# The convolution's second column group: gate and b tiles by seven products, and the mixed operands' slices asked for sooner

## The chip, the cores and the metric

The kernel runs on one core of a Trainium2 chip. The metric is the device time of one execution in microseconds; a comparison takes the median of several runs. The engines are named as the profile names them: PE (matrix engine), DVE (vector), ACT (scalar), POOL (GpSimd) and SP (which only issues transfers here).

## The reference

Two layers on a residual stream x of 1024 tokens by 1024 features. The first, the one touched here, is a gated short convolution; the second is a dilated attention with three groups of heads and is left as it is.

```python
def short_conv_mixer(h, w_in, w_conv, w_out):
    S = h.shape[1]
    proj = h @ w_in                                   # (S, 4*2048)
    b_gate, c_gate, u, z = jnp.split(proj, 4, axis=-1)
    v = c_gate * u
    vp = jnp.pad(v, ((0, 0), (CONV_K - 1, 0), (0, 0)))
    conv = sum(w_conv[k] * vp[:, k:k + S] for k in range(CONV_K))
    y = b_gate * conv * jax.nn.silu(z)
    return y @ w_out
...
x = x + short_conv_mixer(rms_norm(x, conv_norm), ...)
x = x + dilated_attention_mixer(rms_norm(x, attn_norm), ...)
```

## The kernel before

Everything is computed transposed, features on the 128 partitions and tokens along a row, in two halves of 512 tokens (`hf`). The 2048 columns of the convolution are 16 column groups `e` of 128, and each group has four weight tiles `k`: 0 is u, 1 is the c gate, 2 is z (the SiLU gate) and 3 is b. One weight tile is 128x1024: 1024 input features, 128 columns.

**Precision.** A float32 operand is kept as a high and a low part. A weight tile half goes through `split_w` (L156 to L160): ACT copies the high part (L158), DVE subtracts to get the low part (L159). PE then does three matmuls of 512 columns for each 128x128 block: high by high, high by low, low by high.

**Plain products.** `products(k, hf)` (L361) takes a whole weight tile against one half of the tokens: 8 feature blocks by 3 = 24 matmuls (L368 to L370). So a weight tile takes 48, and a pair of them 96.

**Seven products.** `strassen` takes two weight tiles (a pair) as a 2 by 2 block matrix (upper and lower features, first and second tile) and the tokens likewise, and forms the four results from seven products of 12 matmuls each (L295, L297, L298): 84. For this `prepare` (L256) forms four mixed weights on POOL (L270) and splits seven, and four token operands are mixed as well. Their blocks are `blkd` (T1), `blkc` (T2), `blke` (T3) and `blkf` (T4), each of four slices `i`; plain operands stay in `blka`, `blkb`, `blkf` and `blkg`, so T4 takes a buffer that the plain products of the second half read. The products run in the order 1, 2, 4 (of the pair before), 6, 5, 3 (of the pair before), 7. Product 1 reads `blka`, 2 `blkb`, 6 `blkc`, 5 `blkd`, 7 `blke`. Products 1, 6, 7 and 4 accumulate in one PSUM bank, and ACT copies that bank (L303) after products 1 and 6 before the next one adds to it.

**Mixed operands.** `mixed(T)` (L190) is a generator. Each of its first four steps asks SP for four slices of x (L195) and forms slice `i` of T1, T2 and T3 on DVE and ACT (L201 to L214); the last one splits the four slices of T4. So it must be advanced five times before the seven products may begin.

**Order.** PE's order is that of the code (`manual_schedule`), ACT's too up to the end of group 0. The other queues are set by a scheduler that works with due times; each engine then executes its queue in order. Group 0 is done plainly, mixed with the loading of x and the row statistics (`row_stats`, `row_spread`: an inverse square root by small DVE rows, L63 to L67, then transposes on PE). Group 1 is done plainly too, while `mixed` is advanced; from group 2 on, all pairs run by seven products. `evac` takes a plain result: k = 0 and 1 give v, k = 2 the gate, k = 3 the taps of the convolution and `close` (L353 to L358), which multiplies by b and by the gate and sends the result to HBM.

**Buffers that couple the queues.** Raw weights have two (`wr`), so SP's issue of a weight waits until the tile two before is split. Split halves have eight (`ws`), mixed weights three (`sr`), 128x512 work tiles twelve (`f`), taps three (`g`).

Of the kernel before, what the change touches and what calls it, by code (L numbers as in the profile page):

```python
# [26 lines left out]
NE = E // P  # L27
# [8 lines left out]
def trunk(ctx: ExitStack, tc: tile.TileContext, a, out):  # L36
# [89 lines left out]
    def half(hf):  # L126
        return slice(hf * HALF, hf * HALF + HALF)

    with tc.tile_pool(name="wq", bufs=1) as wq, tc.tile_pool(name="sle", bufs=1) as sle, \
# [11 lines left out]
        def ftile():  # L141
            t = fp.tile([P, HALF], F32, name="f", tag="f", bufs=12)
            return t

        def gtile():
            t = cp.tile([P, HALF], F32, name="g", tag="g", bufs=3)
            return t
# [42 lines left out]
        def mixed(T):  # L190


            def x_tile(hf, kt):
                t = ftile()
                nc.sync.dma_start(t, a["x"][hf, kt])  # L195
                return t

            def put(n, i, t):
                if i == 0:
                    T[n] = block(" dcef"[n])  # L200
                nc.scalar.activation(T[n][:, i, 0], t, AF.Copy)  # L201
                nc.vector.tensor_tensor(T[n][:, i, 1], t, T[n][:, i, 0].bitcast(F32), op=OP.subtract)

            fourth = []
            for i in range(4):
                a11, a12, a22, a21 = (x_tile(hf, kt) for hf, kt in ((0, i), (1, i), (1, i + 4), (0, i + 4)))
                nc.vector.tensor_tensor(a12, a12, a11, op=OP.subtract)
                nc.scalar.activation(a12, a12, AF.Copy, scale=g1[:, i:i + 1])
                put(1, i, a12)
                nc.vector.scalar_tensor_tensor(a22, a22, g1[:, i + 4:i + 5], a12, op0=OP.mult, op1=OP.subtract)  # L210
                put(2, i, a22)
                nc.vector.scalar_tensor_tensor(a11, a11, ng1[:, i:i + 1], a22, op0=OP.mult, op1=OP.add)
                put(3, i, a11)
                nc.vector.scalar_tensor_tensor(a21, a21, g1[:, i + 4:i + 5], a22, op0=OP.mult, op1=OP.subtract)  # L214
                fourth.append(a21)
                yield
            for i in range(4):
                put(4, i, fourth[i])
            yield
# [109 lines left out]
        with tc.tile_pool(name="rp", bufs=1, side="right") as rp, tc.tile_pool(name="cp", bufs=2, side="right") as cp, \  # L329
# [5 lines left out]
            def vb_of(e):  # L335
                if e not in VB:
                    VB[e] = cp.tile([P, 2 + S], F32, name="vb", tag="vb")
                    nc.gpsimd.memset(VB[e][:, 0:2], 0.0)
                return VB[e]

            def gate_z(e, hf, z):
                nc.scalar.activation(z, z, AF.Silu)
                nc.gpsimd.tensor_tensor(z, z, R[:, half(hf)], op=OP.mult)
                SZ[e, hf] = z

            def taps(e, hf):
                t = gtile()
                o, vb = hf * HALF, VB[e]
                nc.scalar.activation(t, vb[:, o:o + HALF], AF.Copy, scale=cw[:, e, 0:1])
                nc.vector.scalar_tensor_tensor(t, vb[:, o + 1:o + 1 + HALF], cw[:, e, 1:2], t, op0=OP.mult, op1=OP.add)  # L350
                nc.vector.scalar_tensor_tensor(t, vb[:, o + 2:o + 2 + HALF], cw[:, e, 2:3], t, op0=OP.mult, op1=OP.add)
                TS[e, hf] = t

            def close(e, hf, b):
                t = TS[e, hf]
                nc.vector.tensor_tensor(t, b, t, op=OP.mult)
                nc.gpsimd.tensor_tensor(t, t, SZ[e, hf], op=OP.mult)
                nc.gpsimd.dma_start(ydc[hf, e], t)  # L358
# [4 lines left out]
            def products(k, hf, pool=cps):  # L363
                ps = pool.tile([P, HALF], F32, name="pp", tag="pp")
                for kt in range(KT):
                    w, b = W[k][kt // 4], B[kt // 4, hf]
                    ws = slice(kt % 4 * P, kt % 4 * P + P)
                    nc.tensor.matmul(ps, w[:, 0, ws], b[:, kt % 4, 0], start=(kt == 0), stop=False)  # L368
                    nc.tensor.matmul(ps, w[:, 0, ws], b[:, kt % 4, 1], start=False, stop=False)  # L369
                    nc.tensor.matmul(ps, w[:, 1, ws], b[:, kt % 4, 0], start=False, stop=(kt == KT - 1))  # L370
                return ps

            def evac(e, k, hf, ps):
                cs = half(hf)
                if k == 0:
                    US[e, hf] = ftile()
                    nc.vector.tensor_tensor(US[e, hf], ps, R2[:, cs], op=OP.mult)
                elif k == 1:
                    nc.vector.tensor_tensor(vb_of(e)[:, 2 + hf * HALF:2 + hf * HALF + HALF], ps, US[e, hf], op=OP.mult)
                elif k == 2:  # L380
                    z = ftile()
                    nc.vector.tensor_tensor(z, ps, R[:, cs], op=OP.mult)
                    gate_z(e, hf, z)
                else:
                    taps(e, hf)
                    close(e, hf, ps)

            def plain_w(e, k, parts):
                r = raw_w(a["conv_w_in"][e, k], parts)
                W[k] = [split_w(r[:, :HALF]), split_w(r[:, HALF:])]  # L390

            with tc.manual_schedule(engines={mybir.EngineType.Activation}):
                ps, T = {}, {}
                mix = mixed(T)
# [23 lines left out]
                    evac(0, k, 1, ps[k, 1])  # L418
                evac(0, 3, 0, ps[3, 0])
                evac(0, 3, 1, products(3, 1))  # L420
            for k in range(4):
                plain_w(1, k, 2)
                if k < 3:
                    next(mix)
                for hf in range(2):
                    evac(1, k, hf, products(k, hf))

            pairs = [(e, pr) for e in range(2, NE) for pr in range(2)]

            def pair(n, w):  # L430

# [69 lines left out]
        with tc.tile_pool(name="ev", bufs=1, side="right", reuse_waits="tile") as ev, tc.tile_pool(name="xb", bufs=1, side="right", reuse_waits="tile") as xb, \  # L501
# [124 lines left out]
            pairs = []  # L626
# [193 lines left out]
    with tc.tile_pool(name="sp", bufs=1, space=PSUM) as sp, tc.tile_pool(name="ptp", bufs=2, space=PSUM) as ptp, \  # L820
# [386 lines left out]
        for r in range(3):  # L1207
            k0 = at[2 * r + 2, 0][0] + LD
            k = k0
# [8 lines left out]
        for kt in range(KT):  # L1218
            k = (at[kt // 2 * 2 + 2, 0][0] + 3 if kt < 6 else len(steps) - 8) + kt % 2
# [7 lines left out]
        k = 0  # L1227
# [110 lines left out]
```

## Time and profile before

| | us |
|---|---|
| median of 3 runs | 1931.74 |
| lowest and highest run | 1931.67, 1938.42 |
| the profiled execution | 1936.95 |
| its span, first to last instruction | 1935.2 |

The conv's input projection lies in the first 640 us of the span, its output projection and the attention's projections up to about 1580, the attention's softmax work and the final projection behind. Per 100 us the matrix engine is busy 100.0 from 100 to 600 us, and 86.5 from 1600 to 1700. The profile's rows give start, duration, engine, line of the kernel, and result and operands by the names of the program. A "<-" in brackets names what ended the idle time before the row. Since PE's rows overlap, the time of a matmul in a sequence is the distance of two starts.

### The profile page before, as it was taken

The numbers are of one execution on the slowest core, as the hardware profiler recorded it, in microseconds if no ns is written. First come the engines' busy times: TensorE is split into PE (matmuls) and PEld (weight loads), VectorE is DVE, ScalarE is ACT, GpSimd is POOL, SyncE is SP. The second block draws the span as 40 slices with busy tenths as digits, with TensorE's granted clock in tenths as the row PEclk, the third lists the DMA queues.
The fourth block names the chain that finished last, engine by engine and source line by source line (L and its number), as shares of the span: only waits on it lengthen the run. The fifth ranks groups of instructions, "written<-read, shape, count | busy, mean of one in ns | idle before, by whom it ended". The sixth has DMA issues, their size and how long they took to land.

```text
span 1935.2 us, 30212 instructions
## 1 busy us (share of the span) xinstructions
PE 1894.8 (98%) x10702; PEld 1550.5 (80%) x10702; DVE 1474.2 (76%) x2798; ACT 878.5 (45%) x2007; POOL 902.4 (47%) x835
## 2 busy tenths in 40 slices
PE   8999999999999999999999999999999998889999
PEld 6888888888888788888888888888888876677777
DVE  6866666566666746698898689868988867879896
ACT  6433333333333544454334433444344428778780
POOL 0356666666665311335555545554545451333240
PEclk9999999999999999999999999999999998999999
DMA  5312223223222756423333333333323356897842
GB/s 192 128 59 83 94 79 101 88 88 95 75 87 87 234 181 215 140 98 114 116 113 104 103 120 110 103 104 120 109 92 115 99 184 209 222 288 237 233 140 88
DMA packets 117800, 253.78 MB, mean 131 GB/s; under 512 B 18494, under 2 KB 23838, under 8 KB 117648
## 3 DMA queue, kind: packets, MB, share of 16 engines
q1 hardware_dynamic: 93280, 176.89, 28.4%
q0 software_dynamic: 24368, 74.95, 12.2%
q8 instruction: 84, 1.38, 0.3%
q14 instruction: 68, 0.56, 0.1%
HBM read 192.53 MB, written 67.64 MB: 134 GB/s over the span
## 4 chain that ended last, share of the span: by engine, by line
PE 89%; DVE 3%; DMA 3%; issue 2%; ACT 1%; POOL 1%; SPq 0%; DVEq 0%; POOLq 0%; ACTq 0%
PE pp L295 22%; PE pp L297 21%; PE pp L298 21%; PE pp L547 3%; PE pp L548 3%; PE pp L546 3%; PE po L976 2%; PE pt L955 2%; DMA nld<-nl 2%; PE pp L368 1%; PE pp L369 1%; PE pp L370 1%; PE ps L929 1%; PE pd L1150 1%; PE pd L1152 1%
## 5 line engine op out<-in xcount | busy, mean ns | idle before, releaser
L159 DVE TENSOR_TENSOR ws<-wr,ws 128x512 fp32r<-128x512 f32 x284 | 294.1, 1037 | 114.8 <-ACT ws L158 113.0
L158 ACT ACTIVATE ws<-wr 128x512 fp32r<-128x512 f32 x284 | 178.3, 630 | 368.0 <-PE pp L298 243.3
L158 ACT ACTIVATE ws<-sr 128x512 fp32r<-128x512 f32 x272 | 170.9, 631 | 346.5 <-PE pp L298 285.7
L159 DVE TENSOR_TENSOR ws<-sr,ws 128x512 fp32r<-128x512 f32 x272 | 225.9, 836 | 84.6 <-ACT ws L158 82.6
L270 POOL TENSOR_TENSOR sr<-wr 128x512 f32<-128x512 f32 x136 | 195.0, 1434 | 198.5 <-DMA wr<-in_conv_w_in 68.0
L307 DVE TENSOR_TENSOR f<-pp,f 128x512 f32<-128x512 f32 x204 | 139.7, 685 | 88.1 <-PE pp L298 80.9
L948 ACT ACTIVATE xs<-xs,nl 128x256 f32<-128x256 f32 (+2 forms) x384 | 160.4, 422 | 0.0
L303 ACT ACTIVATE f<-pp 128x512 f32<-128x512 f32 x228 | 132.5, 581 | 8.3 <-PE pp L298 8.2
L270 POOL TENSOR_TENSOR sr<-wr,sr 128x512 f32<-128x512 f32 x68 | 88.8, 1306 | 75.2 <-issue 53.6
L942 DVE CUSTOM_DVE_ANT_0 xs<-ps,bt 128x256 f32<-128x256 f32 (+2 forms) x384 | 102.8, 325 | 19.3 <-DMA zd<-f 7.2
L295 PE MATMUL pp<-blkf,ws 128*128 128x512 f32 x272 | 108.2, 398 | 0.7 <-ACT f L303 0.7
L295 PE MATMUL pp<-blka,ws 128*128 128x512 f32 x272 | 105.9, 389 | 0.7 <-ACT f L303 0.7
L297 PE MATMUL pp<-blkd,ws 128*128 128x512 f32 x272 | 106.3, 391 | 0.0
L295 PE MATMUL pp<-blkd,ws 128*128 128x512 f32 x272 | 106.2, 390 | 0.0
L295 PE MATMUL pp<-blkb,ws 128*128 128x512 f32 x272 | 106.2, 390 | 0.0
L298 PE MATMUL pp<-blkf,ws 128*128 128x512 f32 x272 | 106.1, 390 | 0.0
L297 PE MATMUL pp<-blkf,ws 128*128 128x512 f32 x272 | 106.0, 390 | 0.0
L298 PE MATMUL pp<-blke,ws 128*128 128x512 f32 x272 | 106.0, 390 | 0.0
L295 PE MATMUL pp<-blkg,ws 128*128 128x512 f32 x272 | 105.9, 389 | 0.0
L295 PE MATMUL pp<-blke,ws 128*128 128x512 f32 x272 | 105.9, 389 | 0.0
L298 PE MATMUL pp<-blkb,ws 128*128 128x512 f32 x272 | 105.8, 389 | 0.0
L298 PE MATMUL pp<-blkd,ws 128*128 128x512 f32 x272 | 105.8, 389 | 0.0
(339 smaller groups left out, 5199.1 us busy)
## 6 DMA issues: line engine op xcount, KB each, us to landing
wr<-in_conv_w_in SPq DMA_DIRECT2D x128, 256.0 KB, 3.2
wr<-in_wqk SPq DMA_DIRECT2D x96, 256.0 KB, 3.3
qkd<-blkc POOLq DMA_DIRECT2D x48, 512.0 KB, 3.7
qk<-qkd SPq DMA_DIRECT2D x48, 512.0 KB, 5.3
wr<-in_conv_w_out SPq DMA_DIRECT2D x64, 256.0 KB, 3.1
f<-in_x SPq DMA_DIRECT2D x48, 256.0 KB, 4.7
wr<-in_wv SPq DMA_DIRECT2D x48, 256.0 KB, 3.1
vd<-blkc POOLq DMA_DIRECT2D x96, 128.0 KB, 2.8
```

The costliest lines, as they stand in the source:

```text
L158: nc.scalar.activation(t[:, 0], src, AF.Copy)
L159: nc.vector.tensor_tensor(t[:, 1], src, t[:, 0].bitcast(F32), op=OP.subtract)
L270: nc.gpsimd.tensor_tensor(t, x, y, op=op)
L295: nc.tensor.matmul(ps, w[:, 0, ws], b[:, k, 0], start=new and k == 0, stop=False, skip_group_check=not new)
L297: nc.tensor.matmul(ps, w[:, 0, ws], b[:, k, 1], start=False, stop=False, skip_group_check=not new)
L298: nc.tensor.matmul(ps, w[:, 1, ws], b[:, k, 0], start=False, stop=end and k == 3, skip_group_check=not new)
L303: nc.scalar.activation(t, ps, AF.Copy)
L307: nc.vector.tensor_tensor(m, ps, m, op=OP.add)
L546: nc.tensor.matmul(ps[dt], w[:, 0, ws], b[:, k, 0], start=(q == k == 0), stop=False)
L547: nc.tensor.matmul(ps[dt], w[:, 0, ws], b[:, k, 1], start=False, stop=False)
L942: nc.vector.tensor_tensor_reduce(out=x, in0=flat[s][:, cols], in1=u["bt"][s][:, bs], op0=OP.add, op1=OP.min, scale=-1.0, scalar=3e38, accu ...
L948: nc.scalar.activation(x, x, AF.Exp, bias=nm, scale=-1.0, accum_out=L)
```

## The change

The plain loop of group 1 handles k = 0 and 1 only, and takes the taps of each half right behind v. The pair (group 1, gate and b) becomes the first of the seven-product pairs. `mixed` is advanced once by the start as before, now twice at k = 0 and once at k = 1 (before: once at each of k = 0, 1 and 2), and the fifth time, as before, by `strassen` when the first pair's weights are prepared.

```diff
-            for k in range(4):
+            for k in range(2):
                 plain_w(1, k, 2)
-                if k < 3:
+                next(mix)
+                if k == 0:
                     next(mix)
                 for hf in range(2):
                     evac(1, k, hf, products(k, hf))
-
-            pairs = [(e, pr) for e in range(2, NE) for pr in range(2)]
+                    if k:
+                        taps(1, hf)
+
+            pairs = [(e, pr) for e in range(1, NE) for pr in range(2)][1:]
```

SP's queue where the slices of x for `mixed` are asked for (`wr` is a raw weight tile, in two transfers; `f` from `in_x` a slice). Before:

```order
L153 DMA wr_652<-in_conv_w_in 128x512 x2
L153 DMA wr_734<-in_conv_w_in 128x512 x2
L153 DMA wr_820<-in_conv_w_in 128x512 x2
L153 DMA wr_893<-in_conv_w_in 128x512 x2
L195 DMA f_469<-in_x 128x512
L195 DMA f_471<-in_x 128x512
```

Now:

```order
L153 DMA wr_671<-in_conv_w_in 128x512 x2
L153 DMA wr_761<-in_conv_w_in 128x512 x2
L153 DMA wr_764<-in_conv_w_in 128x512 x2
L195 DMA f_469<-in_x 128x512
L195 DMA f_471<-in_x 128x512
L195 DMA f_473<-in_x 128x512
```

The first slice stood behind four tiles, group 1's k = 1, 2 and 3 and group 2's first (`wr_893`). Now it stands behind group 1's three; twelve slices follow in a row, then group 2's first tile and the last four.

DVE's queue at the first slices, where the small rows of the second half's inverse square root (`rt`, `rtt`) stand. Before:

```order
L67 SCALAR_TENSOR_TENSOR rt_448<-rtt_449,rt_448 128x4
L65 TENSOR_TENSOR rtt_449<-rt_448 128x4
L66 SCALAR_TENSOR_TENSOR rtt_449<-rtt_449,ms_446 128x4
L67 SCALAR_TENSOR_TENSOR rt_448<-rtt_449,rt_448 128x4
L65 TENSOR_TENSOR rtt_449<-rt_448 128x4
L207 TENSOR_TENSOR f_471<-f_471,f_469 128x512
L66 SCALAR_TENSOR_TENSOR rtt_449<-rtt_449,ms_446 128x4
L67 SCALAR_TENSOR_TENSOR rt_448<-rtt_449,rt_448 128x4
L210 SCALAR_TENSOR_TENSOR f_473<-f_473,conv_norm_65,f_471 128x512
L202 TENSOR_TENSOR blkd_479<-f_471,blkd_479 128x512
```

Now:

```order
L67 SCALAR_TENSOR_TENSOR rt_448<-rtt_449,rt_448 128x4
L207 TENSOR_TENSOR f_471<-f_471,f_469 128x512
L65 TENSOR_TENSOR rtt_449<-rt_448 128x4
L66 SCALAR_TENSOR_TENSOR rtt_449<-rtt_449,ms_446 128x4
L67 SCALAR_TENSOR_TENSOR rt_448<-rtt_449,rt_448 128x4
L65 TENSOR_TENSOR rtt_449<-rt_448 128x4
L66 SCALAR_TENSOR_TENSOR rtt_449<-rtt_449,ms_446 128x4
L210 SCALAR_TENSOR_TENSOR f_473<-f_473,conv_norm_65,f_471 128x512
L67 SCALAR_TENSOR_TENSOR rt_448<-rtt_449,rt_448 128x4
L202 TENSOR_TENSOR blkd_479<-f_471,blkd_479 128x512
```

The slice's first row (L207) moved ahead of four rows of the square root, and L210 ahead of its last (L67).

DVE's queue at the end of the mixed operands, from the fourth slices on (`blkc_483` is T2, `blke_487` T3, `blkf_796` T4, `ws_826` the first weight of the pair that follows). Now:

```order
L214 SCALAR_TENSOR_TENSOR f_686<-f_686,conv_norm_65,f_684 128x512
L202 TENSOR_TENSOR blkd_479<-f_682,blkd_479 128x512
L351 SCALAR_TENSOR_TENSOR g_727<-vb_724,conv_w_68,g_727 128x512
L202 TENSOR_TENSOR blkc_483<-f_684,blkc_483 128x512
L159 TENSOR_TENSOR ws_793<-sr_791,ws_793 128x512
L202 TENSOR_TENSOR blkf_796<-f_475,blkf_796 128x512
L202 TENSOR_TENSOR blkf_796<-f_585,blkf_796 128x512
L202 TENSOR_TENSOR blkf_796<-f_604,blkf_796 128x512
L379 TENSOR_TENSOR vb_724<-pp_731,f_669 128x512
L202 TENSOR_TENSOR blke_487<-f_680,blke_487 128x512
L202 TENSOR_TENSOR blkf_796<-f_686,blkf_796 128x512
L159 TENSOR_TENSOR ws_826<-wr_820,ws_826 128x512
```

Before, the last rows of T2 and T3 stood among the evacuations of k = 2 (L382):

```order
L214 SCALAR_TENSOR_TENSOR f_749<-f_749,conv_norm_65,f_747 128x512
L202 TENSOR_TENSOR blkc_483<-f_747,blkc_483 128x512
L350 SCALAR_TENSOR_TENSOR g_886<-vb_705,conv_w_68,g_886 128x512
L382 TENSOR_TENSOR f_787<-pp_762,R_122 128x512
L202 TENSOR_TENSOR blke_487<-f_743,blke_487 128x512
L351 SCALAR_TENSOR_TENSOR g_886<-vb_705,conv_w_68,g_886 128x512
L159 TENSOR_TENSOR ws_917<-sr_915,ws_917 128x512
L382 TENSOR_TENSOR f_816<-pp_791,R_122 128x512
```

The evacuations of the gate tile left this place, and the four splits of T4 and the first weight of the next pair came up to it.

ACT's queue at the copy of product 1 (`f_818<-pp_805`). Now:

```order
L158 ACTIVATE ws_793<-sr_791 128x512
L201 ACTIVATE blkf_796<-f_475 128x512
L201 ACTIVATE blkf_796<-f_585 128x512
L201 ACTIVATE blkf_796<-f_604 128x512
L201 ACTIVATE blke_487<-f_680 128x512
L201 ACTIVATE blkf_796<-f_686 128x512
L158 ACTIVATE ws_826<-wr_820 128x512
L303 ACTIVATE f_818<-pp_805 128x512
L158 ACTIVATE ws_846<-wr_820 128x512
```

Before, the same place (`f_950<-pp_937`) read:

```order
L158 ACTIVATE ws_925<-sr_923 128x512
L201 ACTIVATE blkf_928<-f_475 128x512
L201 ACTIVATE blkf_928<-f_585 128x512
L201 ACTIVATE blkf_928<-f_667 128x512
L201 ACTIVATE blkf_928<-f_749 128x512
L158 ACTIVATE ws_962<-wr_956 128x512
L303 ACTIVATE f_950<-pp_937 128x512
L158 ACTIVATE ws_980<-wr_956 128x512
```

The copy stands behind the same kinds of rows as before, and now also behind the last slice of T3 (`blke_487<-f_680`).

Behind this stretch the queues of all engines stand as they did. The number of weight transfers and of slices is the same; PE has 12 matmuls fewer, and DVE, ACT and POOL have four, six and six rows more.

## The prediction

> **What bounds the kernel now.** I read the page first: the engine totals, then the chain that ended last. Then I asked which engines the matrix engine (PE) waits for, and opened the timelines between 40 and 105 us, where the edited loop runs.
>
> ```profile
> span 1935.2 us, 30212 instructions
> ...
> PE 1894.8 (98%) x10702; PEld 1550.5 (80%) x10702; DVE 1474.2 (76%) x2798; ACT 878.5 (45%) x2007; POOL 902.4 (47%) x835
> ...
> PE 89%; DVE 3%; DMA 3%; issue 2%; ACT 1%; POOL 1%; SPq 0%; DVEq 0%; POOLq 0%; ACTq 0%
> ```
>
> PE is busy 98% of the span and holds 89% of the chain, so a matmul taken out of a stretch where PE never pauses should come off the end. The waits of PE tell where it does pause:
>
> ```profile
> PE ps L929 <- DVE nl L942: 13.2, 3, 7.5
> PE pt L955 <- DVE pts L866: 10.8, 7, 4.2
> PE pp L368 <- ACT ws L158: 6.6, 1, 6.6
> ...
> PE st L236 <- DVE rt L67: 0.6, 1, 0.6
> ```
>
> The first two lie in the attention after 1600 us, the third is the first weight at the start. In the conv only small ones are left. The stretch of the edit has none:
>
> ```profile
> 52.40:101.50 49.10, 49.10 (x220) 40.64 (x218) 43.22 (x57) 22.26 (x37) 19.26 (x16) 1.00 0.30 99
> 57.96 0.39 PE L368 MATMUL pp<-blka,ws 128*128 128x512 f32 x1
> 79.72 0.39 PE L368 MATMUL pp<-blka,ws 128*128 128x512 f32 x1
> 101.48 0.39 PE L295 MATMUL pp<-blka,ws 128*128 128x512 f32 x1
> ```
>
> The first row is the stage table (PE, weight load, DVE, ACT, POOL, clock): PE is busy all 49.10 us at full clock. Below it are the first matmuls of column group 1, of its k = 2, and of the first seven-product pair. Group 1 takes 101.48 - 57.96 = 43.52 us for 8 x 24 = 192 matmuls, 0.2267 us each. A row's 0.39 us is its latency and is not the price.
>
> **The change, term by term.**
>
> **1. Twelve matmuls go.** Gate and b of group 1 took 4 x 24 = 96 matmuls, and take 7 x 12 = 84 now. 12 x 0.2267 = **-2.72 us**, all on PE's path.
>
> **2. The wait for row statistics.** PE stood 0.6 us for the second half's inverse square root (L67). DVE reached it late because an idle wait for the first slices of x stands before:
>
> ```profile
> 45.83 0.43 SPq L195 DMA_DIRECT2D f<-in_x  x1
> 40.91 0.80 SPq L153 DMA_DIRECT2D wr<-in_conv_w_in  x2
> ...
> 48.86 0.17 DVE L67 SCALAR_TENSOR_TENSOR rt<-rtt,rt 128x4 f32<-128x4 f32 x1
> 50.91 0.69 DVE L207 TENSOR_TENSOR f<-f 128x512 f32<-128x512 f32 x1 [1.10 <-DMA f<-in_x]
> ...
> wr<-in_conv_w_in SPq DMA_DIRECT2D x128, 256.0 KB, 3.2
> ...
> f<-in_x SPq DMA_DIRECT2D x48, 256.0 KB, 4.7
> ...
> 51.71 0.16 DVE L67 SCALAR_TENSOR_TENSOR rt<-rtt,rt 128x4 f32<-128x4 f32 x1
> ```
>
> SP asked for x at 45.83, behind four weight tiles. In the new order it does so behind three, the last of which went out at 40.91: some 4 us sooner. With 4.7 us from issue to landing (the page's list of issues) x is there by about 47, so DVE's 1.10 us idle goes. Against that, the new order puts L207 and L210 ahead of rows of the square root, and POOL's first three mixtures (1.3 us each, from the landing of the third tile, 41.3 + 3.2) fall at about 44.5 to 48.5, beside these rows. Ends: -0.6 (wait gone) and +0.6 (twice as long); I take **0**, the middle, since both effects are about one DVE row.
>
> **3. New deadlines.** The seven products begin 4 x 24 matmuls sooner: p1 at 79.72, p2 at 82.44, p6 at 85.16, p5 at 87.88, p7 at 90.60, the next pair at 93.32. The last slice of a block is needed 9 matmuls (2.04 us) into its product: blkc by 87.20, blke by 92.64. In the profile they came at:
>
> ```profile
> 87.80 0.68 DVE L202 TENSOR_TENSOR blkc<-f,blkc 128x512 fp32r<-128x512 f32 x1
> 89.67 0.67 DVE L202 TENSOR_TENSOR blke<-f,blke 128x512 fp32r<-128x512 f32 x1
> ```
>
> At the old pace blkc (88.48) would be late by 1.3 us. What does the new DVE queue make of it? The old stretch, from the first L207 to this blkc, is this row of the stage table:
>
> ```profile
> 50.90:88.50 37.60, 36.96 (x166) 30.37 (x165) 36.24 (x51) 18.20 (x29) 12.14 (x10) 1.00 0.36 117
> 76.03 0.75 DVE L210 SCALAR_TENSOR_TENSOR f<-f,conv_norm 128x512 f32<-128x512 f32 x1 [0.79 <-ACT f L208]
> ```
>
> Of its 51 rows 48 are 128x512 ones wholly inside, two are of 4 columns (some 0.2 us each), the last is cut off at 0.1: (36.24 - 0.4 - 0.1) / 48 = 0.745 us a row, POOL's interference included; 37.60 - 36.24 = 1.4 us is idle. The new queue has, from L207 to the last blkc, also 51 rows, six of them small: 45 x 0.745 + 6 x 0.2 = 34.7 us, and up to 1.4 idle. It starts between 49.1 (x has landed, and the row just ahead is the L67 of 48.86) and 50.9 (as now). So blkc is done between 83.8 and 87.0, **before 87.20**. The last blke stands 6 rows behind (+4.5: 88.3 to 91.5, needed 92.64), and the next pair's first weight 2 more (89.8 to 93.0, needed 93.32).
>
> The interference is inside 0.745, and varies:
>
> ```profile
> 58.30 1.30 POOL L343 TENSOR_TENSOR f<-f,R 128x512 f32<-128x512 f32 x1 [9.50 <-ACT f L342]
> 58.67 1.48 DVE L207 TENSOR_TENSOR f<-f 128x512 f32<-128x512 f32 x1
> 65.86 1.78 DVE L214 SCALAR_TENSOR_TENSOR f<-f,conv_norm 128x512 f32<-128x512 f32 x1
> 67.56 0.68 DVE L377 TENSOR_TENSOR f<-pp,sqacc 128x512 f32<-128x512 f32 x1
> ```
>
> A DVE row that meets a POOL row ends with it: 1.48 instead of 0.69, 1.78 instead of 0.75 (the L210 above). L377, which reads one operand from PSUM, was not lengthened beside POOL. POOL gains four mixtures (L270) and two products; two or three of them (the following pair's) may fall before 87 us, at up to 1.03 us each.
>
> The Trainium skill has a rule for this ("SBUF — State Buffer", section "Who interferes with whom"): a VectorE instruction with two SBUF inputs and a GpSimd instruction that reads SBUF exclude each other for a whole instruction. These rows agree. By that rule two more mixtures would cost DVE about 2 us; without it nothing.
>
> A narrower gate is ACT. p6 writes into p1's bank, so it waits for ACT's copy of p1 (L303), and ahead of that copy now stand a blkf copy, which needs a DVE row three before the last blkc, and a weight's high part.
>
> ```profile
> 99.56 2.19 ACT L201 ACTIVATE blkf<-f 128x512 fp32r<-128x512 f32 x4
> 101.68 0.63 ACT L158 ACTIVATE ws<-wr 128x512 fp32r<-128x512 f32 x1
> 104.40 0.60 ACT L303 ACTIVATE f<-pp 128x512 f32<-128x512 f32 x1 [2.09 <-PE pp L298]
> ```
>
> In the profile the same copies were done 2.09 us before p1. Now that DVE row ends 2.2 us ahead of blkc, at 81.6 to 84.8; with 0.55 + 0.53 + 0.60 behind it the copy is done at 83.3 to 86.5, against 85.16. So PE stands **0 to 1.3 us** before p6; the middle of the walk (84.9) just holds. I take **+0.4**, because the middle leaves only 0.3 us. These waits don't add up: once PE has stood, every later deadline moves with it.
>
> **4. Other engines.** The same weights are loaded, and behind this stretch each engine's order is the old one. ACT's three more splits and three copies (0.6 us each) lie in stretches where it is half idle; POOL's six rows (8 us) where it was busy 19.26 of 49.10. Without that cover they would show as lateness in 3. Closing gate and b moves past DVE's mixtures; PE needs neither result before the output projection.
>
> **Sum**: -2.72 + 0 + 0.4 = -2.3 us. The profiled execution took 1936.95 us (span 1935.2 and 1.75 around it), so 1934.6 of it. That execution lies 5.2 us above the median shown, inside the runs' spread (1931.67 to 1938.42); against the median the time is 1931.74 - 2.3 = **1929.4 us**. That is 0.12%; a measurement of this kernel can tell about 0.5% (9.7 us) from no change.
>
> **Rivals.**
>
> *The statistics come sooner too.* If the x slices' earlier landing shows in L67, term 2 is -0.6 and term 3 zero: -3.3, **1928.4**. For it: DVE's 1.10 us idle. Against: three POOL rows at that place.
>
> *The gain is taken back.* DVE keeps only part of its lead and p6 waits about as long as was saved: net 0, **1931.7**. It needs the copy of p1 done at 87.9, so blkc at 88.4, the old time: the slices' earlier request would have brought nothing. Against: the x slices are the wait that began DVE's late run. For it:
>
> ```profile
> 55.00:80.00 25.00, 24.21 (x33) 1.00 0.40 126
> ```
>
> DVE was busy 24.21 of the 25 us from 55 to 80 and has no slack to make up a late start.
>
> *Slower: DVE's mixtures overrun.* If DVE starts at 50.9, idles 1.4 and every one of three further POOL rows costs it 1.03, blkc is done at 90.1, the copy of p1 at 50.9 + 34.7 + 1.4 + 3.1 - 2.2 + 1.7 = 89.6: PE stands 4.4 us, net +1.7, **1933.4**. It decides where the wait exceeds 2.72 us. For it: the fourth slices are asked for only when POOL has closed group 0, and POOL closes later if its mixtures stand ahead. Against: in the profile that request stood 7.0 us for POOL, and L207's only wait for a DMA was still the first, of 1.1 us.
>
> ```profile
> SPq L195 <- POOL g L357: 7.0, 2, 4.4
> ...
>   DVE f L207: 1.1, 1
> ...
> 1580.00:1600.00 20.00, 12.27 (x62) 9.28 (x60) 4.51 (x10) 3.93 (x7) 7.37 (x10) 0.90 0.67 246
> ```
>
> *The same with a slower clock.* The last row shows a stretch where PE was busy 12.27 of 20 us: its granted clock was 0.90, where it was 1.00 in the edited stretch. A stall of 4.4 us could bring this here: 10% of 20 us is 2 us more, **1935.4**. The Trainium skill ("TensorE: Matmul & The Clock Gate", Part 1, "What's actually happening") says that PE falls to half its clock after an idle window of about 3.4 us. By that rule a stall below it would cost only itself, and this row agrees in direction.
>
> **How the numbers follow.** The forecast (PE stands 0 to 1.3 us, net -1.4 to -2.7) 0.58; statistics sooner 0.18; gain taken back 0.12; slower 0.07; slower with the clock 0.04; outside these 0.01. The range holds the first four: from 1928.4, less 1.2 for what two rows of DVE may shift, to 1933.4, plus 2.6 for the spread that the three runs show upward (6.7 us at the worst, mostly left out): 1927.2 to 1936.0. Every case's price lies within 0.5%. Of the slower cases' 0.11 I count 0.02 as past 9.7 us, and the 0.01 outside as faster by over 0.5%: faster 0.01, same 0.97, slower 0.02.
>
> **What would show it.** PE's first L295 at about 79.7 instead of 101.48, then 84 matmuls of that pair; the conv's end 2 to 3 us sooner. A wait of L295 on ACT f L303 at about 85 us shows term 3, one on blkc or blke the DVE overrun; the wait on rt L67 shows term 2. Wrong would be: a PE wait over 2.7 us there, or a clock below 1.00 before 100 us; or waits of the attention (L929, L955) that grow by what was saved.

## The result and the profile after

| | before | after |
|---|---|---|
| median of the compared runs, us | 1935.31 (6 runs, 1931.67 to 1938.89) | 1926.08 (6 runs, 1923.73 to 1926.98) |
| the profiled execution, us | 1936.95 | 1926.98 |

The ratio is 0.9949, with a 95% interval of 0.9935 to 0.9962: about 9 us less, where the forecast was 2.3. The first lines of the page after (the summary of the profiled execution):

```profile
span 1925.2 us, 30209 instructions
...
PE 1893.2 (98%) x10690; PEld 1548.4 (80%) x10690; DVE 1485.2 (77%) x2802; ACT 879.9 (46%) x2013; POOL 909.9 (47%) x841
```

The 12 matmuls are gone (10702 to 10690), but PE's busy time fell by 1.6 us only, while the span fell by 10.0. So most of what went is idle time of PE. The waits of PE after:

```profile
PE pt L958 <- DVE pts L869: 8.5, 5, 4.4
PE pp L368 <- ACT ws L158: 6.6, 1, 6.6
PE ps L932 <- DVE nl L945: 5.3, 3, 4.2
...
PE pp L295 <- ACT f L303: 1.4, 2, 0.7
PE st L236 <- DVE rt L67: 1.1, 1, 1.1
```

The wait on `nl` (L942 before, L945 now, since the file grew by three lines) still occurs three times, but takes 5.3 us instead of 13.2, and the wait of 7.5 is not among them. That is in the attention, some 1500 us behind the edit. Where along the span does the difference arise? Laying the same rows of both traces beside each other cuts the span into five stretches, in us:

```
                                                     before    after   difference
first matmul to product 1 of the first L295 pair      94.92    74.13    -20.79
from there to the last matmul of the conv projection 537.45   557.10    +19.65
from there to the last attention projection product  952.43   952.16     -0.27
from there to the first softmax row of DVE (xs, nl)    8.36     1.35     -7.01
from there to the end                                335.46   333.84     -1.62
```

The first two belong together: product 1 now comes a pair sooner, and 84 matmuls more follow it. Their sum, **-1.14 us**, is what went up to the end of the conv projection, the edited stretch included. The fourth, **-7.01 us**, is one place. The timeline of before there (start, duration, engine, line, operation, result and operands, and in brackets the idle time before and what ended it):

```profile
1591.78 0.69 DVE L307 TENSOR_TENSOR f<-pp,f 128x512 f32<-128x512 f32 x1 [0.28 <-PE pp L298]
1592.56 1.25 POOL L692 TENSOR_TENSOR f<-f,sqacc 128x512 f32<-128x512 f32 x1 [1.30 <-DVE f L307]
1593.84 0.63 ACT L693 ACTIVATE f<-f 128x512 f32<-128x512 f32 x1 [3.43 <-POOL f L692]
1594.77 0.57 POOL L694 DMA_DIRECT2D zd<-f  x1 [0.96 <-ACT f L693]
...
1599.51 1.28 ACT L948 ACT_TABLE_LOAD   x1 [5.04 <-DMA zd<-f]
1599.72 0.29 DVE L942 CUSTOM_DVE_ANT_0 xs<-ps,bt 128x128 f32<-128x128 f32 x1 [7.25 <-DMA zd<-f]
...
1600.41 1.60 PE L929 MATMUL ps<-qk 64*64 64x192 f32 x16 [7.46 <-DVE nl L942]
```

And after:

```profile
1590.45 0.69 DVE L307 TENSOR_TENSOR f<-pp,f 128x512 f32<-128x512 f32 x1 [0.28 <-PE pp L298]
...
1591.37 0.29 DVE L945 CUSTOM_DVE_ANT_0 xs<-ps,bt 128x128 f32<-128x128 f32 x1 [0.23 <-PE ps L932]
...
1592.07 1.09 PE L932 MATMUL ps<-qk 64*64 64x192 f32 x16 [0.45 <-DVE nl L945]
...
1593.45 0.57 POOL L697 DMA_DIRECT2D zd<-f  x1 [0.96 <-ACT f L696]
```

In both, the last result of the attention's projections goes through DVE (L307), POOL and ACT and is stored to HBM (`zd<-f`). Before, DVE's first softmax row waits for that store to land: it starts 4.95 us after the store was issued, and PE stands 7.46 us. After, the row starts at 1591.37, two microseconds before the store is even issued. Yet the softmax row has neither `f` nor `zd` among its operands. And the change doesn't touch this code.

**Why it waits.** The softmax row also writes the small tile `nl` (its name in the waits). In the placement of both programs (the addresses that their tiles are given when the kernel is built), the first `nl` tile lies on bytes 224992 to 225120 of each partition. The twelve buffers of `f`, which the projections use up to the last store, stand from 204736 on, 2048 bytes each: buffer 9 (counted from 0) has the bytes 223168 to 225216. So `nl` lies on buffer 9, and its first use has to wait until what reads that buffer is done. The tiles of `f` do not take the buffers in a fixed cycle; the buffers that the last eight stores read are

```
before   0  1 11  4  2  7  5  9
after    9  4  8  3 11  6 10  0
```

Before, the last store of all reads buffer 9. The change takes one `f` tile more (the gate and b of group 1 by seven products: 455 tiles instead of 454) and moves the order in which buffers are taken and come free. Which buffer a tile gets is called the rotation below, and it shifts from there on. Now buffer 9 is last read by the eighth store from the end, which was issued at 1559.20 us, 32 us before the softmax row. The instruction's own waits say the same (POOL's transfers are signalled on eight semaphores in turn, and each adds 16 to its semaphore's count):

```
before  L942 xs,nl<-ps,bt 128x128   waits DMASW2 at 464 (the last store), DMAHW6, DVE, PE, Activation
after   L945 xs,nl<-ps,bt 128x128   waits DMASW1 at 432 (the eighth from the end), DMAHW6, DVE, PE
```

So the row waits in both for the last store that reads the buffer under `nl`, and only the age of that store differs. That is read from two programs, and could be a companion of another cause. The experiments make and unmake it.

### The profile page after: what moved, and what is told of

It reads as the page before. It is cut to its first block, busy times and chain, and to the rows that moved or that the text cites. A ratio compares the mean times of both kernels' runs of the same rounds, so it can differ in the third digit from the quotient of the medians.

```text
span 1925.2 us, 30209 instructions
## 1 busy us (share of the span) xinstructions
PE 1893.2 (98%) x10690; PEld 1548.4 (80%) x10690; DVE 1485.2 (77%) x2802; ACT 879.9 (46%) x2013; POOL 909.9 (47%) x841
## 5 line engine op out<-in xcount | busy, mean ns | idle before, releaser
L270 POOL TENSOR_TENSOR sr<-wr 128x512 f32<-128x512 f32 x138 | 193.8, 1404 | 252.7 <-DMA wr<-in_conv_w_in 112.9
L159 DVE TENSOR_TENSOR ws<-sr,ws 128x512 fp32r<-128x512 f32 x276 | 234.2, 855 | 84.7 <-ACT ws L158 82.5
L307 DVE TENSOR_TENSOR f<-pp,f 128x512 f32<-128x512 f32 x207 | 141.6, 684 | 80.8 <-PE pp L298 74.4
L303 ACT ACTIVATE f<-pp 128x512 f32<-128x512 f32 x231 | 134.1, 580 | 5.6 <-PE pp L298 5.3
L270 POOL TENSOR_TENSOR sr<-wr,sr 128x512 f32<-128x512 f32 x69 | 90.5, 1312 | 59.3 <-issue 49.9
L945 DVE CUSTOM_DVE_ANT_0 xs<-ps,bt 128x256 f32<-128x256 f32 (+2 forms) x384 | 102.8, 325 | 12.1 <-PE ps L932 4.7
L295 PE MATMUL pp<-blkf,ws 128*128 128x512 f32 x276 | 109.8, 398 | 0.7 <-ACT f L303 0.7
L297 PE MATMUL pp<-blkd,ws 128*128 128x512 f32 x276 | 107.9, 391 | 0.0
L295 PE MATMUL pp<-blke,ws 128*128 128x512 f32 x276 | 107.7, 390 | 0.1
L295 PE MATMUL pp<-blkd,ws 128*128 128x512 f32 x276 | 107.7, 390 | 0.0
L298 PE MATMUL pp<-blkf,ws 128*128 128x512 f32 x276 | 107.7, 390 | 0.0
L297 PE MATMUL pp<-blkf,ws 128*128 128x512 f32 x276 | 107.6, 390 | 0.0
L298 PE MATMUL pp<-blke,ws 128*128 128x512 f32 x276 | 107.6, 390 | 0.0
L297 PE MATMUL pp<-blke,ws 128*128 128x512 f32 x276 | 107.4, 389 | 0.0
```

The lines of the kernel that those rows point to most:

```text
L159: nc.vector.tensor_tensor(t[:, 1], src, t[:, 0].bitcast(F32), op=OP.subtract)
L270: nc.gpsimd.tensor_tensor(t, x, y, op=op)
L295: nc.tensor.matmul(ps, w[:, 0, ws], b[:, k, 0], start=new and k == 0, stop=False, skip_group_check=not new)
L297: nc.tensor.matmul(ps, w[:, 0, ws], b[:, k, 1], start=False, stop=False, skip_group_check=not new)
L298: nc.tensor.matmul(ps, w[:, 1, ws], b[:, k, 0], start=False, stop=end and k == 3, skip_group_check=not new)
L303: nc.scalar.activation(t, ps, AF.Copy)
```

## The experiments

The theory (**coincidence**): some 8 us hang on whether the last store reads `f` buffer 9, and nothing of the edit is needed for it. The main rival (**work**): they come from the saved matmuls or from the slices asked for sooner, with all that follows them along the span. In the first four kernels, N dummy tiles of `f` are taken, each with a memset of two columns on POOL, so that only the rotation moves. They shared 23 runs of the kernel before (median 1937.04); the last three shared 11 (1937.24).

**One tile more in the kernel before.** No matmul is saved, no slice moved. The last store comes to read buffer 1.

```diff
+            for _ in range(1):
+                nc.gpsimd.memset(ftile()[:, 0:2], 0.0)
             strassen([[a["conv_w_in"][e, 2 * pr + i] for i in range(2)] for e, pr in pairs], pair, between,
```

> The kernel before with one work tile f more taken (and two of its columns set to zero on POOL) ahead of the first seven-product pair; nothing of the change. The order of all queues is that of before but for this one row. It moves which of the twelve f buffers the last z store (L694) reads: from buffer 9, on whose bytes the attention's first nl tile lies, to buffer 1. Theory A (address coincidence: the attention's first DVE row waits for that store's landing): that wait of 7.25 us goes and the time falls by 5 to 9 us against before, to about 1926 to 1930. Theory B (the saved matmuls shift the phase of everything behind, and with it transfers and clock): nothing is shifted here, so the time is that of before, ratio 1.000, and the wait stays.

Measured: 1927.93 (5 runs), ratio 0.9955 with 0.9941 to 0.9968. The first softmax row in its timeline:

```profile
1591.88 0.29 DVE L944 CUSTOM_DVE_ANT_0 xs<-ps,bt 128x128 f32<-128x128 f32 x1 [0.23 <-PE ps L931]
```

One dummy tile brings as much as the whole change, within the intervals. The order of rows on PE, DVE, ACT and SP is the one of before, so work doesn't explain that.

**Two tiles more in the kernel before.** The same edit with `range(2)`; the last store reads buffer 9 again.

> The same with two f tiles more. Here the last z store reads buffer 9 again, under the nl tile. Theory A: the wait of some 7 us is there and the time is that of before, within 0.15%. Theory B: as before too. Theory C (any more f tile, or the memset itself, speeds it up): faster by as much as the run with one tile.

Measured: 1936.96 (12 runs), ratio 1.0004 with 0.9993 to 1.0014, and the wait is back:

```profile
1593.60 0.58 POOL L696 DMA_DIRECT2D zd<-f  x1 [0.96 <-ACT f L695]
...
1600.20 0.29 DVE L944 CUSTOM_DVE_ANT_0 xs<-ps,bt 128x128 f32<-128x128 f32 x1 [8.90 <-DMA zd<-f]
```

So it isn't the added row that helps, but which buffer comes last.

**Nine tiles more in the changed kernel.** Here the dummy tiles stand ahead of the attention's projections, and bring the last store back to buffer 9, with the change in full.

```diff
+            for _ in range(9):
+                nc.gpsimd.memset(ftile()[:, 0:2], 0.0)
             strassen([sources(p) for p in pairs], pair, between, lambda: None)
```

> The changed kernel with nine f tiles more taken (two columns each set to zero on POOL, about 1 us of POOL in all) ahead of the attention's projection. The whole change is in. The last z store reads buffer 9, under the nl tile, as in before. Theory A: the first attention row waits for it again, the time is 5 to 9 us above the changed kernel's, 1931 to 1935, and against before only the 1 to 2 us of the convolution remain (ratio 0.999). Theory B: as the changed kernel, about 1926, ratio 0.995.

Measured: 1936.73 (11 runs), ratio 1.0001 with 0.9991 to 1.001, some 2 us more than was expected. The whole gain of the change is gone:

```profile
1601.91 0.29 DVE L947 CUSTOM_DVE_ANT_0 xs<-ps,bt 128x128 f32<-128x128 f32 x1 [9.21 <-DMA zd<-f]
```

It isn't a clean measure of the edit's own share: the attention's projections took 954.00 us against after's 952.16, with more waits of PE for ACT's copies (L303) where the memsets stand.

**Six tiles more in the changed kernel.** The control, with `range(6)`: about as many added rows, but the last store reads buffer 8.

> The changed kernel with six f tiles more at the same place; the last z store reads buffer 8, not under the nl tile. Theory A: as the changed kernel, about 1926, ratio 0.995. Theory B: the same. If it is as slow as the run with nine, the added rows themselves cost the time and theory A falls.

Measured: 1929.01 (6 runs, 3 us above the changed kernel), ratio 0.9957 with 0.9941 to 0.9972; the projections are longer still (955.12), and the first softmax row doesn't wait:

```profile
1594.05 0.29 DVE L947 CUSTOM_DVE_ANT_0 xs<-ps,bt 128x128 f32<-128x128 f32 x1 [0.23 <-PE ps L934]
```

The memsets cost up to 3 us in that stretch and don't make the difference between nine and six; the buffer does.

**A spacer in the kernel before.** All rotations stay as they are (the last store reads buffer 9), but `nl` moves by 2304 bytes, onto buffer 11 (five small tiles placed behind it move along). The queues are those of before with one POOL row added.

```diff
+        spacer = sm.tile([P, 576], F32, name="spacer", tag="spacer", bufs=1)
+        nc.gpsimd.memset(spacer[:, 0:2], 0.0)
         def parts_tile():
```

> The kernel before with a spacer tile of 2304 bytes ahead of the small attention tiles, so that nl begins 2304 bytes higher, on f buffer 11 instead of 9. No f buffer, no matmul and no queue order is changed but for one small memset on POOL. The last z store still reads buffer 9. Theory A (address coincidence): the first attention row no longer waits for that store; the time falls by 5 to 9 us, ratio 0.9953 to 0.9975. Rival (it is the choice of f buffer, not the nl tile on it, that costs): the time is that of before, ratio 1.000.

Measured: 1928.36 (5 runs), ratio 0.9953 with 0.9941 to 0.9965. This is the most direct of the runs: the same store from the same buffer, and another address for `nl`. The first softmax row stands 1.35 us behind the last product, as in after, and starts while POOL is still at work on the result that the last store sends:

```profile
1594.25 1.26 POOL L692 TENSOR_TENSOR f<-f,sqacc 128x512 f32<-128x512 f32 x1 [1.30 <-DVE f L307]
1594.39 0.29 DVE L945 CUSTOM_DVE_ANT_0 xs<-ps,bt 128x128 f32<-128x128 f32 x1 [0.23 <-PE ps L932]
```

In this program the row waits for the store that reads buffer 11, the sixth from the end.

**The slices sooner, without the seven products.** Group 1 stays plain; `mixed` is advanced as in the change, as far as that goes.

```diff
-                if k < 3:
+                if k < 2:
+                    next(mix)
+                if k == 0:
                     next(mix)
```

> Half of the change: the mixed operands are advanced twice at k = 0 and once at k = 1 of group 1, but all four weight tiles of group 1 stay plain products, so that no matmul is saved. Here the last z store happens to read f buffer 5. Theory A: the whole of the 5 to 9 us comes without a matmul saved, ratio 0.9953 to 0.9975; PE's last product of the conv's input projection is within 0.5 us of before, counted from its first matmul (632.0 us in the mean of three runs). Rival (the gain needs the saved matmuls): ratio 1.000.

Measured: 1927.47 (6 runs), ratio 0.9948 with 0.9935 to 0.996, with all 10702 matmuls. This edit changes the rotation too, though it takes no `f` tile more (454, as before): the last store reads buffer 5, and the first softmax row stands 1.35 us behind the last product. The conv projection doesn't end sooner: 633.79 us after PE's first matmul. That is outside the 0.5 us around 632.0 that was expected, but the kernels with the order of before already lie between 631.66 and 634.46. So its gain lies at that place, not at the slices.

**The statistics first.** In the changed kernel, the start's step of `mixed` moves behind the second half's row statistics.

```diff
-                next(mix)
                 ps[3, 0] = products(3, 0, pp)
                 row_spread(1)
+                next(mix)
```

> The changed kernel with the first step of the mixed operands advanced behind the second half's row statistics instead of ahead of them, so that the rows of the inverse square root stand ahead of the first slice on DVE. The last z store reads f buffer 4. If the wait of 1.1 us for rt (L67) in the changed kernel comes from that order and from POOL's mixtures beside it, it falls to 0.6 or less, and the conv's input projection ends 0.5 us sooner, counted from PE's first matmul (631.1 in the mean of three runs); the mixed operands are some 1 us later and PE then stands up to 1 us more before the products 6 and 7, which may take it back. Total: as the changed kernel within 0.1%, ratio against before 0.994 to 0.996.

Measured: 1927.26 (6 runs), ratio 0.9947 with 0.9935 to 0.996. Against after that is no difference. Its waits of PE up to 120 us:

```profile
PE pp L295 <- ACT f L303: 2.7, 1, 2.7
...
PE st L236 <- DVE rt L67: 0.7, 1, 0.7
```

The edit does less than was meant: on DVE the slice's first row (L207, at 48.78 us) still stands between the rows of the square root. The statistics' wait shrinks from 1.1 to 0.7, where 0.6 or less was expected, but the mixed operands are ready later and PE stands 2.7 us before product 6. From product 1 to the projection's end it takes 559.58 us, against 557.10 in after, and that end comes 631.41 us after PE's first matmul, not 0.5 us sooner than the changed kernel's 631.23.

The stretches of all profiled executions, in us (the columns are those of the five stretches above):

```
                    last store   to p1   p1 to   attention    to first   to the
                    reads                end of  projections  softmax    end
                                         conv                 row
before                   9       94.92   537.45    952.43       8.36     335.46
two tiles more           9       94.21   537.45    951.65      10.02     333.85
one tile more            1       94.33   537.45    952.12       1.35     334.29
spacer                   9*      97.01   537.45    952.10       1.35     333.14
slices sooner alone      5       96.35   537.44    952.58       1.35     332.17
after                    0       74.13   557.10    952.16       1.35     333.84
after, nine more         9       73.74   557.19    954.00      10.33     332.31
after, six more          8       74.02   557.06    955.12       1.35     333.66
statistics first         4       71.83   559.58    952.10       1.35     331.66
* nl moved off buffer 9
```

The fifth column takes two values and nothing between: 1.35 us in six kernels, and 8.36 to 10.33 in the three whose last store reads the bytes under `nl`. The place is worth **7.0 to 9.0 us**. The last column varies by 4 us without following it, and the first by 3 us between the four kernels whose order is that of before; what makes these vary wasn't found. Up to the end of the conv projection (the first two columns together) the four kernels with the group's gate and b by seven products take 630.93 to 631.41 us, and the five without 631.66 to 634.46. So every one with the change ends there sooner, by an amount that this scatter doesn't fix.

## Why the prediction was wrong

**Where it failed.** Step 4, "behind this stretch each engine's order is the old one", is true, and the sum took from it that nothing behind the stretch changes. The order is not all that one stretch hands to the next. The places of tiles in memory are also handed on, and they changed. The step that failed is that inference, and with it the first waits row that the prediction quoted: `nl`'s 13.2 us were taken as part of the attention, and named only as what might grow. Over half of them was a single wait of 7.5 us, and the page of before names what ended it:

```profile
L942 DVE CUSTOM_DVE_ANT_0 xs<-ps,bt 128x256 f32<-128x256 f32 (+2 forms) x384 | 102.8, 325 | 19.3 <-DMA zd<-f 7.2
```

The softmax row was released by a store of something that is not an operand of it. Here that meant that the two share bytes; the question to ask was what decides which ones. The prediction even quoted PE's 12.27 busy us from 1580 to 1600, the same wait, as evidence on the clock alone. No rival covered it, so the range ended above the result.

**Term 1, twelve matmuls, -2.72.** The count is right. Over the stretch behind product 1, 84 matmuls more should add 84 x 0.2267 = 19.04 us; they added 19.65. The 0.6 us are two short stalls (below).

**Term 2, the statistics, 0 between -0.6 and +0.6.** The wait grew from 0.6 to 1.1 us: the upper part of the range. That the edit made it grow isn't shown, since the three kernels with the order of before and a dummy row have 0.6, 0.8 and 1.4 us. The timeline of after does show the mechanism that the prediction held against a gain:

```profile
46.68 1.30 POOL L270 TENSOR_TENSOR sr<-sr,wr 128x512 f32<-128x512 f32 x1
47.94 1.29 POOL L270 TENSOR_TENSOR sr<-wr 128x512 f32<-128x512 f32 x1
48.04 1.21 DVE L65 TENSOR_TENSOR rtt<-rt 128x4 f32<-128x4 f32 x1
49.28 1.22 DVE L66 SCALAR_TENSOR_TENSOR rtt<-rtt,ms 128x4 f32<-128x4 f32 x1
...
51.22 0.16 DVE L65 TENSOR_TENSOR rtt<-rt 128x4 f32<-128x4 f32 x1
...
53.07 0.62 PE L236 MATMUL st<-ident,rt 128*128 128x128 f32 x4 [1.12 <-DVE rt L67]
...
80.76 0.39 PE L295 MATMUL pp<-blka,ws 128*128 128x512 f32 x1
...
85.17 0.58 ACT L303 ACTIVATE f<-pp 128x512 f32<-128x512 f32 x1
85.26 0.68 DVE L202 TENSOR_TENSOR blkc<-f,blkc 128x512 fp32r<-128x512 f32 x1
...
86.20 0.39 PE L295 MATMUL pp<-blkc,ws 128*128 128x512 f32 x1
...
89.97 0.68 DVE L202 TENSOR_TENSOR blke<-f,blke 128x512 fp32r<-128x512 f32 x1
90.13 0.73 ACT L349 ACTIVATE g<-vb,conv_w 128x512 f32<-128x512 f32 x1 [3.86 <-issue]
90.76 0.61 ACT L158 ACTIVATE ws<-sr 128x512 fp32r<-128x512 f32 x1
91.28 0.58 ACT L303 ACTIVATE f<-pp 128x512 f32<-128x512 f32 x1
91.91 0.50 PE L295 MATMUL pp<-blke,ws 128*128 128x512 f32 x1
```

POOL's mixtures (L270) run from 45.14 on, one after the other. Two small rows of DVE, 0.16 us each when alone, take 1.21 and 1.22 and end within 0.02 us of a POOL row beside them (49.25 and 50.50; the next POOL row, L343, ends at 50.48). Before, one of them was so lengthened (L66, 1.15 us). The wide rows that the prediction quoted do not end with the POOL row, as it says, but later: 58.67 + 1.48 = 60.15, against 58.30 + 1.30 = 59.60. The x slices did come early: L207's wait of 1.10 us for them is gone.

**Term 3, the deadlines, +0.4.** The size came out at 0.6, the place was another. The last `blkc` ended at 85.94 (83.8 to 87.0 was predicted), the last `blke` at 90.65 (88.3 to 91.5), ACT's copy of product 1 at 85.75 (83.3 to 86.5). Product 1 itself began 1.04 us later than predicted, at 80.76; so product 6 at 86.20 found the copy done, and PE did not stand there. It stood 0.4 us before product 7, for ACT's second copy, which had the taps (L349) and a weight's split ahead of it, and 0.2 at 130 us, before the next pair's product 7. The gate that the prediction named, ACT's copy behind the mixtures, is shown by the run with the statistics first: there it ended later (86.62 us, with product 6 due at 83.82), and PE stood 2.7 us for it.

**The edit's own sum.** Before product 1, 96 matmuls fewer should take 21.76 us away; 20.79 went, so 0.97 was given back. Of it 0.48 is the statistics (1.12 instead of 0.64). A wait of 0.63 us for the first block of x, at 8.93 us, more than covers the rest; it stands ahead of all that the change moves, the run with the statistics first hasn't got it, and the spacer's kernel, without the change, has one of 0.6. So the edit's own effect, read from these two profiles, is -2.72 + 0.61 + 0.48 = **-1.6 us**, where the forecast had -2.3; it is an estimate, since the 0.48 is within what the wait varies without the edit. By total times this share can't be told from nothing: the intervals of the kernel with one dummy tile (0.9941 to 0.9968) and of the changed one (0.9935 to 0.9962) overlap.

**The rivals.** "Statistics sooner" had the x slices right, but the wait on L67 grew instead of going. "Gain taken back" held for 0.61 + 0.48 of the 2.72 us, and by other waits than the one it named. "Slower" did not occur, and the clock stayed at 1.00 up to 101.50 us. What came was none of them.

## What to carry to other kernels

When a wait's releaser is not an operand of the waiting row, look for shared bytes: a tile of the next stage lies where the last stage's buffer is still being read. Which buffer comes last hangs on how many tiles are taken before and in which order they come free, so an edit that takes one more, or only moves their order (the slices sooner), can switch such a wait on or off, and be credited or blamed for it. Before believing a gain that appears far from its edit, take one dummy tile more in both versions, or move the waiting tile by a spacer; and where a stage's first small tile matters, keep it off the buffers that the last stage stores from.

## What the runs showed of the hardware

**The clock behind the wait.** The stage table from 1600 to 1620 us (busy time of PE, weight load, DVE, ACT and POOL, then the clock), of before:

```profile
1600.00:1620.00 20.00, 18.76 (x233) 14.24 (x234) 15.08 (x80) 17.34 (x68) 1.95 (x3) 0.84 0.48 157
```

and of after:

```profile
1600.00:1620.00 20.00, 20.00 (x294) 16.09 (x292) 15.80 (x90) 18.71 (x85) 2.82 (x5) 1.00 0.70 233
```

With two tiles more (a wait of 9.1 us) it was 0.79, with nine more (9.4 us) 0.75, and 1.00 with one tile more. Windows of 2 us show the step in before, where PE did nothing from 1592.95 to 1600.41:

```profile
1594.00:1596.00 2.00, 0.00 (x0) 0.00 (x0) 0.00 (x0) 0.47 (x1) 0.57 (x1) 1.00 0.14 35
1598.00:1600.00 2.00, 0.00 (x0) 0.00 (x0) 0.28 (x3) 0.49 (x1) 0.00 (x0) 0.50 1.03 419
1604.00:1606.00 2.00, 2.00 (x16) 1.35 (x14) 1.56 (x9) 0.74 (x5) 0.00 (x0) 0.50 0.00 0
1608.00:1610.00 2.00, 2.00 (x24) 1.76 (x25) 2.00 (x13) 2.00 (x8) 0.00 (x0) 1.00 0.36 96
```

The clock is halved some 3 us into the wait and stays so for about 6 us after PE has work again. The Trainium skill ("TensorE: Matmul & The Clock Gate", Part 1, "What's actually happening") has PE fall to half its clock after an idle window of about 3.4 us; this step comes close to it. A long wait isn't needed for it, though. After has 0.57 from 1596 to 1600, with no idle time of PE above 0.66 us from 1590 to 1596, and six tiles more has 0.93 from 1600 to 1620; what made the clock fall there wasn't found. The slower stretch behind the wait costs little in the end: from the first softmax row on, before took 335.46 us, but the two other kernels with the wait took 333.85 and 332.31, no longer than those without.

**A store's landing.** From the last store's issue to the row that waited for it passed 4.95 us before, 6.60 with two tiles more and 6.92 with nine more. The profile's list of transfers has a median of 3.2 us for this group of 16 stores before. Why the last one takes longer wasn't tried.
